# Folded weights kept in DRAM as high and low parts: a hybrid decoder trunk on one Trainium2 core

## The chip, the cores and the metric

The kernel runs on one core of one Trainium2 chip. The metric is the device time of one execution in microseconds. The kernel before took 2501.79 us as the median of 3 runs (2500.89 to 2510.75).

## The reference

One decoder layer on x of 2048 tokens by 1024 columns, in f32, with 256 memory tokens for cross-attention:

```python
mem_n = rmsnorm(mem, mem_norm_g)
h = rmsnorm(x, mix_norm_g)
q, k, v, g, u = split(h @ w_in)                       # 5 x 512 columns
y_ret  = silu(g) * head_rmsnorm(retention(q, k, v))   # 4 heads, chunks of 128, rotary on q and k
y_pool = pool_mixer(u, pool_w, pool_scale)            # 4 groups, causal windows 2/4/8/16, a linear each
x = x + concat(y_ret, y_pool) @ w_out
x = x + cross_attn(rmsnorm(x, xa_norm_g), mem_n, wq, wkv, wo)   # 4 heads of 256
x = x + conv_glu_ffn(rmsnorm(x, ffn_norm_g), w_up, conv_w, conv_b, w_down)
out = rmsnorm(x, final_norm_g)
```

Three products of weights can be made ahead, as the activations come in linearly on one side: wq with the keys of a head (q k^T = h (wq k^T)), the values of a head with wo, and the pooling linear with the rows of w_out behind it. The kernel calls this folding.

## The kernel before, in words

**Tokens and products.** The 2048 tokens are worked in two halves b of T = 1024. Activations lie transposed, 128 columns of the model on the partitions and tokens along the free axis. Every large product has its f32 inputs kept as two f32r numbers, a high and a low part, and takes three matmuls (`passes`, L239: high x high on L241, high x low on L242, low x high on L243). `split` (L230) makes the two parts: a ScalarE copy rounds to the high part (L233, or L236 with a scale), and VectorE subtracts it for the low part (L216, or L225 with a scale). A `unit` (L285) is one output tile of 128 rows by 1024 tokens: it takes a weight tile of 128 x 1024, splits its two halves (`pairs`, L255) and runs 48 matmuls of 512 columns into two PSUM banks, a half weight tile at a time.

**Places.** In SBUF there are five raw tiles R for weights as they are loaded (`new_raw`, L245), three places Q for half a weight tile as a pair (`new_pair`, L250), ten slots T of 576 columns for all kinds of temporaries (`TT`), eight slots Z, and a large arena G for x and 16 further slots (B). PSUM has five banks `mm` for large products and three for the rest (`aux`). A place is taken and freed in program order; the tile framework puts in the waits, by which the next writer of a place stands behind its last reader. A transfer out of a place is a reader too, until it has landed.

**Order.** The framework's scheduler orders the instructions of the whole program by a simulated timeline; each engine then works its own queue in that order. Transfers are issued from SP's queue (nearly all loads), ScalarE's (stores of results) and POOL's. The sums of feed-forward weights (`weight_sums`, L903) are made in DRAM beside the rest by transfers from SP and POOL.

**Folding** (`folded_weights`, L360) is a generator that runs beside the first half's mixing, a piece at a time between the units of a retention head (L1518, L1521). After the projections of the memory to keys and values:
- Md (L460 to L478): for each head, four products of 512 columns (two tiles of 256) of wq^T and keys, 12 matmuls of 256 columns each. ScalarE scales them out of PSUM into a slot of T (L472) and `keep` (L431) stores the slot to DRAM, 256 KB. 16 such tiles.
- VWd (L480 to L496): for each head, four products of 512 columns, 6 matmuls each, of values and wo; evacuated on L490 and stored by `keep`. 16 tiles.
- WPd (L504 to L516): for each pooling group, two products of 512 columns of the pooling linear and its rows of w_out; L511 and `keep`. 8 tiles.

**Use.** Behind the four heads and the pooling groups comes the out-projection (L1534): eight units, whose weight tile is half w_out (L1536) and half WPd (L1537), loaded into the two halves of one raw tile. Then `attention` (L822): `load_m` (L830) loads Md, 512 KB at a time for two tiles, and splits them into two regions of G and Z, except for the first two tiles, whose pairs lie in Q; the products with M, the softmax on tiles of 128 tokens and transposes (L850) follow. Then eight units with VWd (L1576), each a load of 512 KB by `load_tile` (L303) that is split by the unit. Both halves of the tokens load all three again.

Of the kernel before, what the change touches and what calls it, by code (L numbers as in the profile page):

```python
# [8 lines left out]
F32 = mybir.dt.float32  # L9
# [6 lines left out]
P = 128  # L16
# [103 lines left out]
def trunk(ctx, tc, xT, memT, pos, w_qkgu, w_v, wkv, wqT, wo, wout_r, wout_p, poolT, w_up, w_dn, vecs, consts, outT):  # L120
# [72 lines left out]
    Md = drp.tile([2, KT, P, SUB], F32, tag="Md", name="Md")  # L193
    VWd = drp.tile([KT, P, KT, P], F32, tag="VWd", name="VWd")
    rope_d = drp.tile([2, P, SUB], F32, tag="rope_d", name="rope_d")
    WPd = drp.tile([KT, P, 4, P], F32, tag="WPd", name="WPd")
# [67 lines left out]

    def rsqrt(y, v):

        t = small(v.shape[1])
        ts(dve, y.bitcast(I32), v.bitcast(I32), -0.5, ALU.mult, 1597463007.0, ALU.add)
        for _ in range(3):
            tt(dve, t, y, y, ALU.mult)  # L270
            stt(t, t, -0.5, v, ALU.mult, ALU.mult)
            stt(y, t, 1.5, y, ALU.add, ALU.mult)
# [12 lines left out]
    def unit(raw, rhs, evac, order=range(4)):  # L285


        hs = pairs(raw)
        ps = [mmps() for _ in range(NS)]
        for h in range(2):  # L290
            for s in range(NS):
                for j, kk in enumerate(order):
                    k = 4 * h + kk
                    w = [hs[h][:, i, kk * P : (kk + 1) * P] for i in range(2)]
                    passes(ps[s], w, rhs(k, s), h + j == 0, h == 1 and j == 3)
                next(behind[0], None)
                quarter[0] += 1
                if not slow[0] or quarter[0] % 2:
                    next(under[0], None)
                if h == 1:  # L300
                    evac(s, ps[s])
# [58 lines left out]
    def folded_weights():  # L360
# [70 lines left out]
        def keep(dst, t, n):  # L431
            act.dma_start(dst, t.f[:, :SUB].rearrange("p (n c) -> p n c", n=n))
            t.free()

        def tiles4(d, nh, k):
            return d[4 * nh : 4 * nh + 4, :, k, :].rearrange("n p c -> p n c")
# [23 lines left out]
        for h in range(HEADS):  # L460
            dp = [row_pairs(wqT[(2 * h + dt) * P : (2 * h + dt + 1) * P, :]) for dt in range(2)]
            for k2 in range(KT // 2):
# [6 lines left out]
                t = TT.take()  # L469
                for j in range(2):  # L470
                    k = 2 * k2 + j
                    act.activation(t.f[:, j * NMEM : (j + 1) * NMEM], ps[:, j * NMEM : (j + 1) * NMEM], AF.Identity, scale=xag[:, k : k + 1])  # L472
                keep(Md[h // 2, 2 * k2 : 2 * k2 + 2, :, (h % 2) * NMEM : (h % 2 + 1) * NMEM].rearrange("k p m -> p k m"), t, 2)
# [6 lines left out]
        for h in range(HEADS):  # L480
            dp = [row_pairs(wo[(2 * h + dt) * P : (2 * h + dt + 1) * P, :]) for dt in range(2)]
            for mt in range(2):
                for nh in range(2):
# [5 lines left out]
                    t = TT.take()  # L489
                    act.activation(t.f[:, :SUB], ps, AF.Identity, scale=rn[:, mt : mt + 1])  # L490
                    keep(tiles4(VWd, nh, 2 * h + mt), t, 4)
# [12 lines left out]
        for g in range(4):  # L504
            u = row_pairs(wout_p[g])
            for nh in range(2):
# [3 lines left out]
                t = TT.take()  # L510
                act.activation(t.f[:, :SUB], ps, AF.Copy)  # L511
                keep(tiles4(WPd, nh, g), t, 4)
# [309 lines left out]
    def attention(sums, beside, pace):  # L822
# [7 lines left out]
        def load_m(hp):  # L830

            out = mw[hp]
            for kp in range(KT // 2):
                raw = new_raw()
                fetched[0] = sp.dma_start(raw.rearrange("p (k n) -> p k n", k=2), Md[hp, 2 * kp : 2 * kp + 2].rearrange("k p n -> p k n"))
                if hp == 0 and kp == 0:

                    out += [(pr[:, 0], pr[:, 1]) for pr in pairs(raw)]
                    yield
                    continue  # L840
                for i in range(2):
                    u = third[2 * hp].r[:, (2 * kp + i) * T : (2 * kp + i + 1) * T]
                    split(raw[:, i * SUB : (i + 1) * SUB], u[:, :SUB], u[:, SUB:])
# [655 lines left out]
    for b in range(NB):  # L1499
# [34 lines left out]
        for n in range(KT):  # L1534
            raw = new_raw()
            sp.dma_start(raw[:, :SUB], wout_r[n].rearrange("p k c -> p (k c)"))  # L1536
            fetched[0] = sp.dma_start(raw[:, SUB:], WPd[n].rearrange("p k c -> p (k c)"))  # L1537
# [30 lines left out]
        for n in range(KT):  # L1568
# [7 lines left out]
            unit(load_tile(VWd[n]), rhs, add_residual(b, n, xs, acc=acc[n]))  # L1576
# [150 lines left out]
```

## Time and profile before

| | |
|---|---|
| median of 3 runs | 2501.79 us (2500.89 to 2510.75) |
| profiled execution, device time | 2506.72 us |
| its span, first to last instruction | 2504.9 us |
| granted TensorE clock, mean | 0.992 |
| TensorE (PE) busy | 2442.7 us |
| VectorE (DVE) busy | 1666.9 us |
| ScalarE (ACT) busy | 1216.1 us |
| GpSimd (POOL) busy | 652.4 us |
| moved by the DMA engines | 474.28 MB, 189 GB/s on average |

The profile is that of one execution. Its lines name an engine, a source line (L472 is line 472 of the kernel), the tiles written and read ("T<-mm" writes T from a bank mm), and times in microseconds or, where noted, nanoseconds. A helper's line, such as L216 or L233, stands for all who call it, so the tiles tell them apart. Md is stored at 144.7 to 222.2 us of the span and VWd at 250.9 to 289.9; the loads of Md are issued from 421.2 and those of VWd from 465.9 in the first half of the tokens, and the last of VWd in the second half at 1133.8. The feed-forward part takes the rest of the span.

### The profile page before, as it was taken

How to read it: one execution, taken by the hardware profiler on the slowest of the kernel's cores; microseconds unless marked ns; L12 is line 12 of the kernel's file. 1: busy time of each engine (PE TensorE's matmuls, PEld its weight loads, DVE VectorE, ACT ScalarE, POOL GpSimd, SP SyncE). 2: the span in 40 equal slices, each digit the busy share in tenths (PEclk: the TensorE clock that was granted, in tenths of full speed). 3: DMA queues.
4: the chain of work that ended last, by engine and by line, in shares of the span. 5: the costliest groups of instructions: out<-in, count | busy, mean ns of one | idle time of the engine just before them, and what ended most of it. 6: DMA issues, size and time to landing. Idle time of an engine off the chain costs nothing.

```text
span 2504.9 us, 33172 instructions
## 1 busy us (share of the span) xinstructions
PE 2442.7 (98%) x11390; PEld 2037.7 (81%) x11390; DVE 1666.9 (67%) x2574; ACT 1216.1 (49%) x2163; POOL 652.4 (26%) x579
## 2 busy tenths in 40 slices
PE   6999999999999999999999999999999999999997
PEld 6888887788788888888887888878888887888885
DVE  8646566564635675574678776886677586867875
ACT  6333423343321223434654555665555576666663
POOL 1010122100121120030237352553335154222322
PEclk9999999999999999999999999999999999999998
DMA  8363888715766764366567564755556468768951
GB/s 318 89 168 110 244 191 233 234 40 181 227 152 145 159 158 149 111 221 220 167 205 270 166 203 153 236 192 165 160 160 213 136 220 287 250 185 280 346 164 68
DMA packets 257177, 474.28 MB, mean 189 GB/s; under 512 B 26864, under 2 KB 56176, under 8 KB 257008
## 3 DMA queue, kind: packets, MB, share of 16 engines
q1 hardware_dynamic: 212336, 408.18, 49.0%
q0 software_dynamic: 19584, 34.61, 8.9%
q10 hardware_dynamic: 25088, 29.37, 3.4%
q8 instruction: 89, 1.46, 0.2%
q14 instruction: 80, 0.66, 0.1%
HBM read 370.87 MB, written 170.39 MB: 216 GB/s over the span
## 4 chain that ended last, share of the span: by engine, by line
PE 78%; DMA 8%; DVE 6%; issue 3%; POOL 2%; ACT 2%; SPq 0%; POOLq 0%; ACTq 0%; DVEq 0%
PE mm L241 25%; PE mm L242 24%; PE mm L243 24%; POOL T L216 1%; DVE Z L216 1%; DMA T<-Xd 1%; DVE Z L225 1%; DVE G L216 1%; DMA T<-xT 1%; DVE Q L216 1%; DVE T L216 1%; DMA T<-Gd 1%; POOL Z L216 1%; PE aux L749 1%; DMA R<-VWd 0%
## 5 line engine op out<-in xcount | busy, mean ns | idle before, releaser
L241 PE MATMUL mm<-G,Q 128*128 128x512 f32 (+1 forms) x1888 | 728.1, 386 | 21.8 <-ACT Q L233 11.1
L243 PE MATMUL mm<-G,Q 128*128 128x512 f32 (+1 forms) x1888 | 725.9, 385 | 4.4 <-DVE Q L216 4.2
L242 PE MATMUL mm<-G,Q 128*128 128x512 f32 (+1 forms) x1888 | 725.7, 385 | 0.7 <-DVE G L216 0.7
L241 PE MATMUL mm<-G 128*128 128x512 f32 (+1 forms) x1380 | 532.1, 387 | 10.0 <-DVE Z L216 6.3
L242 PE MATMUL mm<-G 128*128 128x512 f32 (+1 forms) x1380 | 531.7, 386 | 0.0
L243 PE MATMUL mm<-G 128*128 128x512 f32 (+1 forms) x1380 | 531.1, 385 | 0.0
L241 PEld LDWEIGHTS mm<-G,Q 128*128 128x128 f32 x1888 | 357.8, 190 | 91.1 <-ACT Q L233 11.8
L243 PEld LDWEIGHTS mm<-G,Q 128*128 128x128 f32 x1888 | 357.7, 190 | 74.3 <-DVE Q L216 5.9
L242 PEld LDWEIGHTS mm<-G,Q 128*128 128x128 f32 x1888 | 358.0, 190 | 69.4 <-DVE G L216 1.6
L225 DVE SCALAR_TENSOR_TENSOR Z<-Z,vecs 128x1024 f32<-128x1024 f32 x176 | 276.3, 1572 | 153.5 <-ACT Z L1069 145.3
L241 PEld LDWEIGHTS mm<-G 128*128 128x128 f32 x1380 | 260.4, 189 | 64.5 <-DVE Z L216 8.0
L243 PEld LDWEIGHTS mm<-G 128*128 128x128 f32 x1380 | 260.2, 189 | 51.8
L242 PEld LDWEIGHTS mm<-G 128*128 128x128 f32 x1380 | 260.1, 188 | 51.5
L1006 ACT ACTIVATE G<-R 128x512 fp32r<-128x512 f32 (+1 forms) x272 | 166.5, 615 | 197.8 <-PE mm L242 178.6
L216 DVE TENSOR_TENSOR Z<-Z,mm 128x512 f32<-128x512 f32 x284 | 192.8, 679 | 78.2 <-PE mm L243 78.0
L216 DVE TENSOR_TENSOR Q<-R,Q 128x512 fp32r<-128x512 f32 x199 | 148.6, 748 | 143.4 <-ACT Q L233 138.9
L216 POOL TENSOR_TENSOR G<-R,G 128x512 fp32r<-128x512 f32 (+1 forms) x100 | 141.9, 1420 | 376.2 <-ACT G L1006 290.9
L233 ACT ACTIVATE Q<-R 128x512 fp32r<-128x512 f32 x150 | 93.8, 627 | 234.8 <-PE mm L242 187.3
L1006 ACT ACTIVATE Q<-R 128x512 fp32r<-128x512 f32 (+1 forms) x204 | 125.0, 613 | 90.9 <-PE mm L242 73.5
L216 DVE TENSOR_TENSOR G<-R,G 128x512 fp32r<-128x512 f32 (+1 forms) x168 | 131.5, 794 | 46.7 <-ACT G L233 38.0
L216 DVE TENSOR_TENSOR G<-T,G 128x512 fp32r<-128x512 f32 (+1 forms) x168 | 125.4, 758 | 53.9 <-ACT G L955 40.7
L940 ACT ACTIVATE aux<-R 128x512 f32<-128x512 f32 (+1 forms) x184 | 105.8, 576 | 95.8 <-DVE Q L216 52.9
(222 smaller groups left out, 2911.4 us busy)
## 6 DMA issues: line engine op xcount, KB each, us to landing
R<-Ud SPq DMA_DIRECT2D x176, 256.0 KB, 2.7
T<-Gd SPq DMA_DIRECT2D x168, 256.0 KB, 4.1
R<-w_up SPq DMA_DIRECT2D x132, 256.0 KB, 3.1
Gd<-Z SPq DMA_DIRECT2D x110, 256.0 KB, 2.4
Ud<-w_up SPq DMA_DIRECT2D x88, 256.0 KB, 5.9
R<-w_qkgu SPq DMA_DIRECT2D x32, 512.0 KB, 4.4
R<-Dd SPq DMA_DIRECT2D x64, 256.0 KB, 4.0
Gd<-T SPq DMA_DIRECT2D x56, 256.0 KB, 3.1
```

Source lines behind the costliest of these rows:

```text
L216: return eng.tensor_tensor(out=out, in0=a, in1=b, op=op)
L225: dve.scalar_tensor_tensor(out=out, in0=a, scalar=s, in1=b, op0=op0, op1=op1)
L233: act.activation(hi, src, AF.Copy)
L241: pe.matmul(ps, lh, rh, start=start, stop=False, skip_group_check=more)
L242: pe.matmul(ps, lh, rl, start=False, stop=False, skip_group_check=more)
L243: pe.matmul(ps, ll, rh, start=False, stop=stop, skip_group_check=more)
L749: pe.matmul(col(self.kv, c), col(self.kn.f, c), self.ch(v, c, h * T), start=True, stop=True)
L940: act.activation(t, x, AF.Copy)
L1006: act.activation(p2[:, 0, :w], self.raw[i].f[:, :w], AF.Copy)
```

## The change

The split is moved from behind the loads to ahead of the stores. `keep` now takes the PSUM bank, splits it into two slots of T (ScalarE the high part, VectorE the low part, both from PSUM; for Md in two halves, as each has a scale of its own) and stores both slots. Md, VWd and WPd hold pairs in DRAM, twice the bytes. `load_m` loads each M tile's pair, 512 KB, straight into the region or place where the product reads it; the VWd units load two pairs of 512 KB straight into Q, and the out-projection loads its WPd half as a pair into Q and splits only its half of w_out. `unit` takes a list of pairs as it is.

```diff
@@ -190,10 +190,10 @@
     t.free()
     dve.memset(phalo, 0.0)
 
-    Md = drp.tile([2, KT, P, SUB], F32, tag="Md", name="Md")
-    VWd = drp.tile([KT, P, KT, P], F32, tag="VWd", name="VWd")
+    Md = drp.tile([2, KT, P, 2, SUB], F32, tag="Md", name="Md")
+    VWd = drp.tile([KT, 2, P, 2, 4, P], F32, tag="VWd", name="VWd")
     rope_d = drp.tile([2, P, SUB], F32, tag="rope_d", name="rope_d")
-    WPd = drp.tile([KT, P, 4, P], F32, tag="WPd", name="WPd")
+    WPd = drp.tile([KT, P, 2, 4, P], F32, tag="WPd", name="WPd")
 
     def mmps():
         return mmp.tile([P, SUB], F32, tag="mm", name=nm("mm"))
@@ -262,6 +262,11 @@
             out.append(pr)
         return out
 
+    def load_pair(src):
+        pr = new_pair()
+        fetched[0] = sp.dma_start(pr.bitcast(F32), src)
+        return pr
+
     def rsqrt(y, v):
 
         t = small(v.shape[1])
@@ -285,7 +290,7 @@
     def unit(raw, rhs, evac, order=range(4)):
 
 
-        hs = pairs(raw)
+        hs = raw if isinstance(raw, list) else pairs(raw)
         ps = [mmps() for _ in range(NS)]
         for h in range(2):
             for s in range(NS):
@@ -428,12 +433,17 @@
                 split(raw[:, i * SUB : (i + 1) * SUB], u.r[:, i * SUB : (i + 1) * SUB], u.r[:, T + i * SUB : T + (i + 1) * SUB])
             return u
 
-        def keep(dst, t, n):
-            act.dma_start(dst, t.f[:, :SUB].rearrange("p (n c) -> p n c", n=n))
-            t.free()
-
-        def tiles4(d, nh, k):
-            return d[4 * nh : 4 * nh + 4, :, k, :].rearrange("n p c -> p n c")
+        def keep(dsts, ps, n, g=None):
+
+            two = [TT.take() for _ in range(2)]
+            hi, lo = (t.f[:, :SUB].bitcast(F32R) for t in two)
+            w = SUB // n
+            for j in range(n if isinstance(g, list) else 1):
+                at = slice(j * w, (j + 1) * w) if isinstance(g, list) else slice(0, SUB)
+                split(ps[:, at], hi[:, at], lo[:, at], g[j] if isinstance(g, list) else g)
+            for t, dst in zip(two, dsts):
+                act.dma_start(dst, t.f[:, :SUB].rearrange("p (n c) -> p n c", n=n))
+                t.free()
 
         kk = B.take(4)
         kp4 = kk.r.rearrange("p (n i m) -> p n i m", i=2, m=NMEM)
@@ -466,11 +476,8 @@
                         k = 2 * k2 + j
                         w = [dp[dt].r[:, i * T + k * P : i * T + (k + 1) * P] for i in range(2)]
                         passes(ps[:, j * NMEM : (j + 1) * NMEM], w, (kp4[:, 2 * h + dt, 0], kp4[:, 2 * h + dt, 1]), dt == 0, dt == 1)
-                t = TT.take()
-                for j in range(2):
-                    k = 2 * k2 + j
-                    act.activation(t.f[:, j * NMEM : (j + 1) * NMEM], ps[:, j * NMEM : (j + 1) * NMEM], AF.Identity, scale=xag[:, k : k + 1])
-                keep(Md[h // 2, 2 * k2 : 2 * k2 + 2, :, (h % 2) * NMEM : (h % 2 + 1) * NMEM].rearrange("k p m -> p k m"), t, 2)
+                to = Md[h // 2, 2 * k2 : 2 * k2 + 2, :, :, (h % 2) * NMEM : (h % 2 + 1) * NMEM]
+                keep([to[:, :, i].rearrange("k p m -> p k m") for i in range(2)], ps, 2, [xag[:, 2 * k2 + j : 2 * k2 + j + 1] for j in range(2)])
             for u in dp:
                 u.free()
             if h == HEADS - 1:
@@ -486,9 +493,8 @@
                         lh = [vp4[:, 2 * h + dt, i, mt * P : (mt + 1) * P] for i in range(2)]
                         w = [dp[dt].r[:, i * T + nh * SUB : i * T + (nh + 1) * SUB] for i in range(2)]
                         passes(ps, lh, w, dt == 0, dt == 1)
-                    t = TT.take()
-                    act.activation(t.f[:, :SUB], ps, AF.Identity, scale=rn[:, mt : mt + 1])
-                    keep(tiles4(VWd, nh, 2 * h + mt), t, 4)
+                    to = VWd[4 * nh : 4 * nh + 4, h // 2, :, :, 2 * (h % 2) + mt]
+                    keep([to[:, :, i].rearrange("n p c -> p n c") for i in range(2)], ps, 4, rn[:, mt : mt + 1])
             for u in dp:
                 u.free()
             if h == HEADS - 1:
@@ -507,9 +513,8 @@
                 ps = mmps()
                 lh = [pw.r[:, i * SUB + g * P : i * SUB + (g + 1) * P] for i in range(2)]
                 passes(ps, lh, [u.r[:, i * T + nh * SUB : i * T + (nh + 1) * SUB] for i in range(2)], True, True)
-                t = TT.take()
-                act.activation(t.f[:, :SUB], ps, AF.Copy)
-                keep(tiles4(WPd, nh, g), t, 4)
+                to = WPd[4 * nh : 4 * nh + 4, :, :, g]
+                keep([to[:, :, i].rearrange("n p c -> p n c") for i in range(2)], ps, 4)
             u.free()
             if g == 3:
                 pw.free()
@@ -831,16 +836,13 @@
 
             out = mw[hp]
             for kp in range(KT // 2):
-                raw = new_raw()
-                fetched[0] = sp.dma_start(raw.rearrange("p (k n) -> p k n", k=2), Md[hp, 2 * kp : 2 * kp + 2].rearrange("k p n -> p k n"))
-                if hp == 0 and kp == 0:
-
-                    out += [(pr[:, 0], pr[:, 1]) for pr in pairs(raw)]
-                    yield
-                    continue
-                for i in range(2):
-                    u = third[2 * hp].r[:, (2 * kp + i) * T : (2 * kp + i + 1) * T]
-                    split(raw[:, i * SUB : (i + 1) * SUB], u[:, :SUB], u[:, SUB:])
+                for k in (2 * kp, 2 * kp + 1):
+                    if hp == 0 and kp == 0:
+                        pr = load_pair(Md[hp, k])
+                        out.append((pr[:, 0], pr[:, 1]))
+                        continue
+                    u = third[2 * hp].r[:, k * T : (k + 1) * T]
+                    fetched[0] = sp.dma_start(u.bitcast(F32), Md[hp, k].rearrange("p i n -> p (i n)"))
                     out.append((u[:, :SUB], u[:, SUB:]))
                 yield
 
@@ -1534,7 +1536,9 @@
         for n in range(KT):
             raw = new_raw()
             sp.dma_start(raw[:, :SUB], wout_r[n].rearrange("p k c -> p (k c)"))
-            fetched[0] = sp.dma_start(raw[:, SUB:], WPd[n].rearrange("p k c -> p (k c)"))
+            pr = new_pair()
+            split(raw[:, :SUB], pr[:, 0], pr[:, 1])
+            raw = [pr, load_pair(WPd[n].rearrange("p i k c -> p i (k c)"))]
             got, ahead = ahead, fetch_x(b, n + 1) if n + 1 < KT else None
             unit(raw, lambda k, s: (mix[k].r[:, s * SUB : (s + 1) * SUB], mix[k].r[:, T + s * SUB : T + (s + 1) * SUB]), add_residual(b, n, xs, got=got), (0, 2, 3, 1))
         for u in mix:
@@ -1573,7 +1577,7 @@
                 at = (k % 4) * T + s * SUB
                 return tuple(prob[k // 4].r[:, i * 4 * T + at : i * 4 * T + at + SUB] for i in range(2))
 
-            unit(load_tile(VWd[n]), rhs, add_residual(b, n, xs, acc=acc[n]))
+            unit([load_pair(VWd[n, h].rearrange("p i k c -> p i (k c)")) for h in range(2)], rhs, add_residual(b, n, xs, acc=acc[n]))
             act.dma_start(Xd[b, n], acc[n].f)
             if b + 1 < NB:
                 load_x(n, nxt, got)
```

## The prediction

> **What bounds the kernel now.** I read the page's first part, then the whole list of TensorE's waits, then the stretches in which TensorE idles.
>
> ```profile
> span 2504.9 us, 33172 instructions
> ...
> PE 2442.7 (98%) x11390; PEld 2037.7 (81%) x11390; DVE 1666.9 (67%) x2574; ACT 1216.1 (49%) x2163; POOL 652.4 (26%) x579
> ```
> TensorE is busy for 2442.7 of 2504.9 us, so 62.2 us are idle in all. The change leaves the matmuls as they are; it can save a part of those 62 us, or add to them.
>
> ```profile
> engine line waited for: us in total, times, longest us
> PE mm L241 <- ACT Q L233: 11.1, 4, 9.0
> ...
> PE aux L850 <- DVE T L220: 4.5, 2, 4.3
> ...
> PE aux L777 <- DVE T L216: 0.8, 2, 0.5
> PE mm L242 <- DVE G L216: 0.7, 1, 0.7
> PE mm L241 <- ACT T L490: 0.3, 1, 0.3
> PE aux L749 <- ACT T L744: 0.2, 1, 0.2
> ```
> Each row is an engine and line, what it waited for, the sum, the number of times and the longest. The 11.1 us lie at the very start and are not touched. Around the folding (100 to 340 us) TensorE waits only for the last rows, 0.5 + 0.3 + 0.2 = 1.0 us: today's folding is all but free. The 4.3 us of L850 are the entry of attention of the first half of the tokens, and those the change can reach:
>
> ```profile
> 500.96 1.11 PE L850 MATMUL aux<-consts,T 128*128 128x128 f32 x4 [4.34 <-DVE T L220]
> ...
> 502.30 0.63 PE L243 MATMUL mm<-G 128*128 128x512 f32 x1
> 502.73 0.63 PE L241 MATMUL mm<-G 128*128 128x512 f32 x1
> ...
> 504.12 0.39 PE L242 MATMUL mm<-G 128*128 128x512 f32 x1
> 504.35 0.39 PE L243 MATMUL mm<-G 128*128 128x512 f32 x1
> ```
> ```profile
> 481.77 12.46 DMA R<-VWd
> ```
> ```profile
> ACT Q L233 <- DMA R<-VWd: 11.2, 1, 11.2
> ```
> The chain of waits says why: a load of VWd takes 12.46 us, ScalarE stands before its split for 11.2 us in its in-order queue, and the exponentials of the softmax are queued behind it. After the gap TensorE starts matmuls every 0.43 us instead of 0.23 for about 3 us, which costs some seven matmuls at 0.2, 1.5 us more.
>
> **The change part by part.** Durations first; columns are the group, busy us and mean ns of one, then idle before it by releaser.
>
> ```profile
> L490 ACT ACTIVATE T<-mm,rnm 128x512 f32<-128x512 f32 x16 | 10.9, 687 | 11.4 <-DMA VWd<-T 6.6 <-PE mm L243 2.2 <-ACT T L490 1.4
> L472 ACT ACTIVATE T<-mm,vecs 128x256 f32<-128x256 f32 x32 | 13.3, 473 | 6.0 <-PE mm L243 3.7 <-PE aux L777 2.2
> L225 DVE SCALAR_TENSOR_TENSOR T<-aux,vecs,T 128x512 f32<-128x512 f32 x6 | 4.5, 750 | 1.5 <-PE aux L777 1.4
> L225 DVE SCALAR_TENSOR_TENSOR T<-T,aux 128x128 f32<-128x128 f32 x14 | 4.0, 284 | 0.4
> L233 ACT ACTIVATE G<-R 128x512 fp32r<-128x512 f32 x41 | 24.7, 629 | 22.9 <-DMA R<-wout_p 8.2 <-DMA R<-wo 7.8 <-PE mm L242 4.6
> L216 DVE TENSOR_TENSOR Q<-R,Q 128x512 fp32r<-128x512 f32 x25 | 17.2, 690 | 42.2 <-ACT Q L233 42.0
> ```
> ```profile
> Md<-T ACTq DMA_DIRECT2D x16, 256.0 KB, 2.8
> ```
> ```profile
> R<-Md SPq DMA_DIRECT2D x8, 512.0 KB, 5.6
> R<-VWd SPq DMA_DIRECT2D x5, 512.0 KB, 13.7
> ```
> ```profile
> L432 ACTq DMA_DIRECT2D VWd<-T x16: 366/366/519, 250.9 to 289.9; - x16
> ...
> DMA to landing us min/median/max: 2.3/5.7/17.2
> ```
>
> *Work moved.* Removed are the splits after the loads: 32 for Md, 32 for VWd, 16 for WPd, each one ScalarE operation of 0.63 us and one VectorE operation of 0.69: 50 and 55 us on engines that are 49% and 67% busy. Added in the folding are 32 low parts of 256 columns for Md (no row has this shape; between 0.28 of 128 and 0.75 of 512 columns I take the middle, 0.45), 16 for VWd at 0.75 and 8 for WPd at 0.69: 32 us of VectorE. ScalarE's evacuations stay (L490, L472, L511); it issues 40 more stores, 40 x 0.37 = 15 us. None of this is on TensorE, so it counts only where TensorE waits for it: at three bursts of fold products, at two entries, and at the loads.
>
> *The folding.* A fold product is 6 matmuls of 512 columns (12 of 256 for Md), 6 x 0.23 = 1.4 us, into one of five PSUM banks. Before, one ScalarE operation freed the bank. Now the VectorE low part behind it frees it, and each product takes two slots of the ten of T, each freed only when its store has landed. In the built order of the changed kernel I followed each such wait:
> - Md of the last head: the first product after the head's transposes needs the bank whose low part stands behind a gating operation (0.75), a query split (0.69), half a low part (0.45), the other half's high part (0.47), and its own end (0.45): 2.8, and 0.5 for hand-overs: 3.3 us. Two products later a rotation's VectorE operation waits for a slot whose store was issued 2.8 us (landing) before, about 1; a further bank about 1. **5 us**, from 3 to 7.
> - VWd, first burst of eight: the high part of the fourth product waits for the landing of the second's store, out of the same slot. From the second's high part: 0.69, issue 0.37, landing 5.7, then high 0.69 and low 0.75 = 8.2 us, in which TensorE has 1.44 us of waiting for the previous low part and then one product and four transposes, 1.9: about 4.9 us idle. The next two products wait for low parts queued on VectorE, about 1 more, and the slowed matmuls after a gap of 4.9 us cost 1.5, as behind the gap at 500.96. **7.5 us**. Its 5.7 is the median of the last row (VWd's stores and loads). With 2.3, the least there, the gap is 1.5 and there is no slow stretch: 2.5. With twice the median it is 13.
> - VWd, second burst: its slots have a head's whole unit more; nothing unless a landing passes 8 us.
> - WPd: five products in a row wait for low parts that stand among the last head's rotation and gating, some behind a landing. By the same queues **4 us**, from 1 to 6.
>
> Sum 16.5, less the 1.0 us of waits that stand there today: +15.5.
>
> How long those stores take decides most of it. The Trainium skill ("DMA: Bandwidth & Descriptors", section "Latency and other measured facts") puts a fixed cost of about 2 us on a small DMA. By it the VWd burst would cost 2.5 and the sum fall by 5; the median row of 5.7 us speaks against it, under the load of this stretch, and the sum goes by the row.
>
> *Entry of attention, first half.* With no split of VWd or Md left, ScalarE doesn't stand before a load there: the 4.3 us gap and its 1.5 us of slow matmuls go, **-5.8**. What is late next: eight 512 KB loads of M pairs for the first two heads go into places that come free as the last out-projection unit ends, 32 to 100 matmuls (7 to 23 us) before their use, at 5.6 us each in the row above, up to several in flight; I take +1.8 (0 to 4). Net **-4**.
>
> *Pool and out-projection, first half.*
>
> ```profile
> 373.64 7.30 DMA Ud<-w_up
> ...
> 384.51 0.49 POOL T L630
> ```
> ```profile
> 385.00:390.00 5.00, 4.46 (x19) 3.14 (x17) 4.88 (x8) 0.00 (x0) 2.55 (x4) 1.00 0.48 56
> 390.00:395.00 5.00, 1.77 (x7) 1.17 (x8) 5.00 (x11) 1.75 (x3) 1.13 (x2) 1.00 1.00 295
> ...
> 620.00:640.00 20.00, 20.00 (x90) 16.57 (x89) 10.94 (x17) 7.66 (x13) 4.15 (x5) 1.00 0.92 229
> ```
> After the stretch and its length stand the busy times of PE, PEld, DVE, ACT and POOL, the granted clock, the share of the DMA engines and GB/s. At 385 to 395 TensorE is busy 6.23 of 10 us: 3.8 idle. The chain runs from a weight sum's transfer (Ud) to POOL's pooling copies (L630), which stand behind the sums in POOL's queue. In the built order fewer sums are ahead of them (28 of their first transfers instead of 40), so most of it goes; but the WPd pairs are twice the bytes and Q holds three, not five, tiles. **-2** (-4 to +3).
>
> *Later loads.* Q's three places let a VWd pair be asked for one unit (48 matmuls, 11 us) ahead; before, five places of R. A 512 KB load within 11 us is in time by the 5.6 us row and late by the 13.7 us row; at 620 to 640 the DMA engines are 0.92 busy, and 4 MB more in the 88 us of this stage (8 units) is 48 GB/s. I take **+1** (0 to 21, the latter 8 units x (13.7 - 11.1)). In the second half the first WPd pair has 22 matmuls, 5 us: **+1.5** (0 to 4).
>
> **Sum:** 15.5 - 4 - 2 + 1 + 1.5 = **+12 us**. The profiled execution took 2506.72 us of device time (1.8 around its span), so 2518.7 like for like; the median of the runs is 2501.79, 4.93 below it, and 2513.8 on that scale. The prediction is **2513.8**, slower by 0.48%.
>
> **The rivals.**
> 1. *The bursts are absorbed and the stall goes: not slower.* If stores land in 2.3 us and the scheduler's interleaving leaves TensorE other work, the folding costs 1 to 3 and -5.8 and -2 stand: -3 to -8, at about 2497. For it: VectorE is 67% busy over the span, and today's folding waits for 1.0 us. Against: five banks, and ten slots that carry rotation and retention as well. It decides from a landing under about 3 us.
> 2. *Pair loads come late.* Double bytes and three places: 8 units x 2.6 = 21 us on top of the forecast, about 2534. For it: 13.7 us and 0.92 busy; against: 13.7 us is the row of five loads asked for close together as attention begins; later ones are spread one unit apart.
> 3. *Nothing that counts.* The removed splits lay beside matmuls, the added low parts do too: within 3 us of before.
> 4. *The clock.* In the Trainium skill ("TensorE: Matmul & The Clock Gate", "What's actually happening") an idle gap of about 3.4 us or more halves TensorE's clock until it has been busy for as long again. The row at 500.96 agrees: 4.34 us idle, then 0.43 us spacing. If the three bursts each pause for over 4.3 us, two more slow stretches of 1.5 us come: +15, about 2517. This lies within the forecast's spread.
>
> **How the numbers follow.** Forecast (with rival 4), from +4 to +24: 0.58, of which 0.25 lies under +12.5. Rival 1: 0.20, of which 0.06 is beyond -12.5. Rival 2: 0.15. Rival 3: 0.07. About 0.5%, 12.5 us, is what a measurement of this kernel can tell from no change; so faster 0.06, same 0.25 + 0.14 + 0.07 = 0.46, slower 0.33 + 0.15 = 0.48. The range runs from -7 (part of rival 1's cases) to +33 (rival 2): 2495 to 2535.
>
> **What would show it.** Right: TensorE's list of waits gains rows for VectorE low parts of fold products (L225 out of mm) or of rotations at 215 to 335 us, some 16 us in all, with stores of VWd and Md behind them; the row of L850 behind L220 with 4.3 us and ScalarE's wait for VWd are gone; 385 to 395 has more than 8 us of matmuls. Wrong: TensorE's waits in the folding stay under 5 us; or TensorE waits for DMAs into Q in the unit loops (rival 2); or the added waits lie elsewhere, in the feed-forward stage for instance, whose order of work the scheduler may have moved.

## The result, and the profile after

The changed kernel takes 2566.67 us (median of 5 runs, 2562.81 to 2573.16), the kernel before 2500.89 (5 runs, 2497.74 to 2510.75): a ratio of 1.0258, 95% interval 1.0231 to 1.0284. It is 66 us slower; forecast was 12 (2513.8 against 2501.79), in a range that ended at 2535.

The page of the profiled execution of the changed kernel (device time 2562.81 us) opens so:

```profile
span 2561.0 us, 33151 instructions
...
PE 2460.4 (96%) x11390; PEld 2046.6 (80%) x11390; DVE 1652.0 (65%) x2550; ACT 1170.8 (46%) x2081; POOL 658.1 (26%) x579
...
DMA packets 276762, 505.75 MB, mean 197 GB/s; under 512 B 28017, under 2 KB 73713, under 8 KB 276593
```
ScalarE does 45 us less and VectorE 15 us less, as the change means to do. TensorE's idle time rose from 62.2 to 2561.0 - 2460.4 = 100.6 us, and its busy time by 17.7 us for the same 11390 matmuls: it ran at a lower clock more often (granted clock 0.984 instead of 0.992 on average). 38.4 + 17.7 = 56.1 us is the whole difference of the two spans.

To see where, take two landmarks that both kernels have: the last store of WPd (the end of the folding) and the first store of x (Xd) behind a VWd unit. Their rows give first and last start; first the kernel before, then the changed one.

```profile
L432 ACTq DMA_DIRECT2D WPd<-T x8: 366/366/562, 314.8 to 332.6; - x8
```
```profile
L1577 ACTq DMA_DIRECT2D Xd<-Z x16: 326/326/327, 592.7 to 1205.0; - x16
```
```profile
L445 ACTq DMA_DIRECT2D WPd<-T x16: 366/366/1308, 333.8 to 358.2; - x16
```
```profile
L1581 ACTq DMA_DIRECT2D Xd<-Z x16: 326/326/349, 646.2 to 1262.3; - x16
```

| part | before | changed | difference |
|---|---|---|---|
| start to last WPd store (folding) | 332.6 | 358.2 | +25.6 |
| from there to the first x store behind VWd (pooling, first out-projection, entry of attention) | 260.1 | 288.0 | +27.9 |
| from there to the last such store (the other VWd units and the second half of the tokens) | 612.3 | 616.1 | +3.8 |
| the rest of the span (feed-forward) | 1299.9 | 1298.7 | -1.2 |

So nearly all of it arises before 650 us, in two parts of about equal size. The first landmark does not cut the work at quite the same place: 1751 matmul instructions lie ahead of it in the changed kernel and 1742 in the one before, and at 0.23 us each for those of 512 columns the 9 more are about 2 us that belong to the second part. In the folding the changed kernel's matmuls show these gaps (in brackets: idle before, and what ended it):

```profile
216.78 0.55 PE L241 MATMUL mm<-G 128*128 128x256 f32 x1 [4.50 <-DVE T L225]
...
219.69 0.41 PE L242 MATMUL mm<-G 128*128 128x256 f32 x1
219.90 0.41 PE L243 MATMUL mm<-G 128*128 128x256 f32 x1
...
220.54 0.28 PE L241 MATMUL mm<-G 128*128 128x256 f32 x1
220.66 0.28 PE L242 MATMUL mm<-G 128*128 128x256 f32 x1
...
263.00 0.50 PE L241 MATMUL mm<-G 128*128 128x512 f32 x1 [1.75 <-DVE T L225]
...
267.25 0.65 PE L782 MATMUL aux<-consts,T 128*128 128x128 f32 x4 [2.58 <-DVE T L216]
...
272.34 0.79 PE L241 MATMUL mm<-G 128*128 128x512 f32 x1 [4.44 <-DVE T L225]
...
277.62 0.63 PE L241 MATMUL mm<-G,Q 128*128 128x512 f32 x1
278.05 0.51 PE L242 MATMUL mm<-G,Q 128*128 128x512 f32 x1
278.39 0.39 PE L243 MATMUL mm<-G,Q 128*128 128x512 f32 x1
278.63 0.39 PE L241 MATMUL mm<-G,Q 128*128 128x512 f32 x1
```
The first is the Md burst, the next three the first VWd burst. Behind the Md gap matmuls of 256 columns come 0.21 us apart instead of 0.12, until 220.12. Behind the last of the VWd burst those of 512 columns come 0.43 us apart until 278.05, so the slow stretch lasts 5.7 us. In the second part it is the first out-projection and the statistics behind it:

```profile
429.15 0.79 PE L241 MATMUL mm<-G,Q 128*128 128x512 f32 x1 [5.49 <-DMA Q<-WPd]
...
461.29 0.79 PE L241 MATMUL mm<-G,Q 128*128 128x512 f32 x1 [7.23 <-ACT Q L233]
...
489.94 0.79 PE L241 MATMUL mm<-G,Q 128*128 128x512 f32 x1 [3.31 <-DMA Q<-WPd]
499.55 0.50 PE L241 MATMUL mm<-G,Q 128*128 128x512 f32 x1 [2.28 <-ACT Q L233]
...
530.65 1.84 PE L320 MATMUL aux<-consts,T 128*128 128x1 f32 x8 [5.24 <-DVE T L216]
```
The gap of 4.34 us at L850 is gone, and larger ones ahead of it have come. The transfers in 390 to 545 us of the changed kernel (number, size, median from issue to landing) and the busy share of the DMA engines in two stretches:

```profile
Ud<-w_up SPq DMA_DIRECT2D x43, 256.0 KB, 11.0
Ud<-w_up POOLq DMA_DIRECT2D x22, 256.0 KB, 8.2
Ud<-Ud POOLq DMA_DIRECT2D x22, 256.0 KB, 12.0
Q<-WPd SPq DMA_DIRECT2D x8, 512.0 KB, 13.9
```
```profile
450.00:460.00 10.00, 4.07 (x18) 3.02 (x17) 1.98 (x3) 1.26 (x2) 1.63 (x2) 0.96 1.09 286
460.00:470.00 10.00, 8.71 (x29) 7.00 (x30) 3.28 (x5) 2.41 (x4) 1.63 (x2) 0.70 1.04 323
```
The last two numbers are the busy share and GB/s: the engines are full (shares a little above 1 stand so in the profile), and a WPd pair that Q's places ask for 11 us ahead takes 13.9. The largest group of transfers is not the pairs at all but the sums of feed-forward weights (Ud), of which the kernel before issues fewer there: 24 from SP in 370 to 500 us, a stretch 25 us shorter.

```profile
Ud<-w_up SPq DMA_DIRECT2D x24, 256.0 KB, 6.3
```
From one landmark to the other it is 36 before and 44 in the changed kernel; between the first and the last WPd load of the changed kernel stand 29. The chain of waits from a WPd load to a matmul that waits for one (start, length, what) runs through SP's queue:

```profile
415.25 13.86 DMA Q<-WPd
...
429.17 12.74 DMA T<-xT
...
441.92 12.42 DMA Ud<-w_up
...
454.36 11.76 DMA Ud<-w_up
...
467.32 7.78 DMA Ud<-w_up
...
475.93 13.97 DMA Q<-WPd
...
489.94 0.79 PE mm L241
```
By these rows, whose releasers the profile infers, SP stands until one transfer has landed before it issues the next, though a load of x (xT) does not read a WPd pair, nor a sum a load of x. In 390 to 545 us SP waits for landings for about 100 of 155 us; in the kernel before, in 370 to 500, for 28 of 130. So a late transfer also delays the next ones in SP's order. How much of the lateness comes from the bytes and how much from this order was not separated by a run.

### The profile page after: what moved, and what is told of

The parts are those of the page before. It is cut to its first block, busy times and chain, and to the rows that moved or that the text cites. A ratio compares the mean times of both kernels' runs of the same rounds, so it can differ in the third digit from the quotient of the medians.

```text
span 2561.0 us, 33151 instructions
## 1 busy us (share of the span) xinstructions
PE 2460.4 (96%) x11390; PEld 2046.6 (80%) x11390; DVE 1652.0 (65%) x2550; ACT 1170.8 (46%) x2081; POOL 658.1 (26%) x579
## 4 chain that ended last, share of the span: by engine, by line
PE 77%; DMA 11%; DVE 5%; issue 3%; POOL 2%; ACT 2%; SPq 1%; POOLq 0%; ACTq 0%; DVEq 0%
PE mm L241 24%; PE mm L242 24%; PE mm L243 24%; DMA T<-xT 2%; DMA Ud<-w_up 2%; POOL T L216 1%; DMA Q<-WPd 1%; DVE Z L216 1%; DVE T L216 1%; DVE G L216 1%; DVE Z L225 1%; DMA VWd<-T 1%; POOL Z L216 1%; DMA T<-Xd 1%; PE aux L743 1%
## 5 line engine op out<-in xcount | busy, mean ns | idle before, releaser
L216 DVE TENSOR_TENSOR Q<-R,Q 128x512 fp32r<-128x512 f32 x147 | 112.0, 763 | 99.7 <-ACT Q L233 88.3
L216 DVE TENSOR_TENSOR G<-T,G 128x512 fp32r<-128x512 f32 (+1 forms) x171 | 131.4, 779 | 62.9 <-ACT G L957 40.5
L216 DVE TENSOR_TENSOR T<-T 128x512 f32<-128x512 f32 (+4 forms) x153 | 107.6, 713 | 75.2 <-ACT T L360 59.9
L216 DVE TENSOR_TENSOR G<-R,G 128x512 fp32r<-128x512 f32 (+1 forms) x156 | 125.7, 817 | 33.1 <-ACT G L233 22.2
```

The source lines that it names most:

```text
L216: return eng.tensor_tensor(out=out, in0=a, in1=b, op=op)
```

## The experiments

Two theories of the out-projection were tried first. **S**: the weight sums, which the scheduler now puts more densely into this part, fill the DMA engines, and everything waits for its bytes. **P**: the WPd pairs themselves, twice as large and through three places of Q, come late. "Stage" below is the time from the last WPd store to the first x store behind VWd. All ratios are to the kernel before on the same chip. Parts and stages are read from one profiled execution each, while executions of one kernel differ by up to 15 us in all (no_low from 2541.17, the profiled one, to 2556.57): a few us between two stages say little.

**One of the three pairs at a time**, and the changed kernel without low parts.

```diff
 md_only:  keep() and load_m as changed; VWd and WPd stored and loaded as before
 vw_only:  VWd alone as changed          wp_only:  WPd alone as changed
```


> Only Md is split ahead of its stores and loaded as pairs; VWd and WPd as in the kernel before. In the built order 32 transfers of weight sums stand between the first and last load of WPd (20 in the kernel before, 29 in the changed one). Theory S (the first out-projection is slow because more of the weight sums' transfers stand in it and fill the DMA engines): out-projection stalls of over 8 us remain, though WPd is loaded as before; 15 to 30 us slower than before. Theory P (it is slow because the WPd pairs are 512 KB each and Q has three places): no stall there, only Md's burst in the folding (about 4.5 us) and M loads: 3 to 10 us slower.

> Only VWd is split ahead of its stores and loaded as pairs. Both theories: the burst in the folding of about 9 us at 260 to 275 us of the span and little in the out-projection, where 20 transfers of sums stand as in the kernel before; the wait of 4.3 us at the entry of attention gone or replaced; 5 to 15 us slower than before. If VWd's pairs come late in their units: over 20.

> Only WPd is split ahead of its stores and loaded as pairs. 24 transfers of sums stand between the first and the last load of WPd. Theory P: TensorE waits for loads of Q from WPd and for splits of w_out behind them, 15 us or more: 18 to 35 us slower than before. Theory S: about 3 us in the folding and under 5 us in the out-projection: 3 to 9 us slower.

| | median us | ratio (95%) | folding ends | stage |
|---|---|---|---|---|
| md_only | 2520.57 | 1.0064 (1.0042 to 1.0086) | 339.7 (+7.1) | 262.9 |
| vw_only | 2529.40 | 1.0103 (1.0077 to 1.0129) | 346.4 (+13.8) | 262.4 |
| wp_only | 2521.26 | 1.0071 (1.0050 to 1.0091) | 340.7 (+8.1) | 260.2 |

The costs in the folding add up: 29.0 against 25.6 together, or some 22 against 24 when the matmuls ahead of the landmark are counted alike (14 more than in the kernel before in vw_only, 16 more in wp_only). The stage doesn't: each alone leaves it at 260 to 263 us. TensorE's waits in wp_only from 390 to 545 us:

```profile
PE aux L320 <- DVE T L216: 6.8, 2, 6.5
PE mm L241 <- DMA Q<-WPd: 3.3, 3, 1.4
```
Late WPd pairs alone cost 3.3 us, so theory P in its simple form is out. md_only stalls 8.1 us in the out-projection though its WPd is loaded as before, as S expected, but the stage as a whole is only 2.8 us longer. vw_only (24.7 us over the kernel before) and wp_only (16.6) came out slower than S had them, and not in the stage: their foldings cost 13.8 and 8.1 us instead of 9 and 3, some 3 and 4 of it by those additional matmuls, and from the first to the last x store behind VWd they take 7.5 and 5.3 us more than the kernel before (619.8 and 617.6 against 612.3). For vw_only more than 20 us was to mean VWd pairs that come late in their units; the trace has one such wait of 4.17 us, at 1151.48.

```diff
 no_low, in keep():
-            two = [TT.take() for _ in range(2)]
...
-                split(ps[:, at], hi[:, at], lo[:, at], ...)
...
+            t = TT.take()
...
+                act.activation(hi[:, at], ps[:, at], AF.Identity, scale=...)   # Copy for WPd
+            for dst in dsts:  # one slot, stored twice
+                act.dma_start(dst, t.f[:, :SUB]...)
```


> The changed kernel without the low parts in the folding: one ScalarE operation evacuates each product into one slot, which is stored twice (the low part that is loaded is thus not the low part). Loads as in the changed kernel. Both theories: the 14 to 16 us of waits of TensorE for low parts and slots at 215 to 355 us go, with some 3 us of slow clock behind them: 15 to 22 us faster than the changed kernel, still 40 to 50 slower than before, as 28 transfers of sums and the pairs of WPd still meet in the out-projection.

2553.92 us, 1.0198 (1.0181 to 1.0216), 15 us less than the changed kernel by the two ratios (0.6%); the last WPd store at 342.9, so 15.3 of the 25.6 us are gone and 10.3 stay. But 25 more matmuls stand ahead of that landmark than in the kernel before (1767 against 1742), which is 5 to 6 us of the 10.3: with no low part in sight, 40 more stores cost some 5 us. The stage stays at 285.3, with those 25 matmuls fewer in it.

**The sums taken out of the out-projection**, in the changed kernel and in the one before.

```diff
 after_hold, before_hold:
+        if b == 0:
+            under, paused = [iter(())], under
         for n in range(KT):
             raw = new_raw()
...
+        if b == 0:
+            under = paused
         for u in mix:
             u.free()
```


> The changed kernel with the generator of the weight sums not called in the eight units of the first out-projection, so that they are made up later. In the built order 9 of their SP transfers stand between the first and last WPd load (29 in the changed kernel) and none between there and the first VWd load. Measure: from the last WPd store to the first store behind a VWd unit, 288 us in the changed kernel, 260 in the one before. Theory S (sums flood the DMA engines in this stage): 260 to 270. Theory P (places of Q and 512 KB pairs): still over 280. The total can get worse at other places, where the sums then stand.

> The kernel before with the same edit: the control. The stage from the last WPd store to the first store behind a VWd unit stays at 255 to 262 us by both theories; the total within 10 us of before.

The stage falls from 288.0 to 253.8 us in the changed kernel, further than S had it, and from 260.1 to 252.1 in the one before, where both theories had it stay; with the sums out, the two kernels differ by 1.7 us (12 matmuls fewer lie in the stage of after_hold, so 4 to 5 at equal work). Pairs of twice the size and three places of Q, without the sums beside them, thus do not make the stage long: P is out. after_hold's total is 2574.43 us, 1.0271 (1.0253 to 1.0289): the sums now meet the second half's WPd and VWd, where a wait for a WPd pair of 10.80 us stands at 992.99, and from the first to the last x store behind VWd it takes 658.8 us instead of 616.1. before_hold is 2501.61, 0.9986 (0.9975 to 0.9997): the only version here that beats the kernel before, and only by 0.14%. The stage of both, in one row each (share of the DMA engines and GB/s last):

```profile
360.20:614.00 253.80, 247.99 (x1158) 204.08 (x1157) 136.98 (x295) 76.85 (x169) 24.40 (x35) 1.00 0.55 175
```
```profile
333.70:585.80 252.10, 249.34 (x1170) 207.26 (x1169) 152.88 (x323) 90.57 (x197) 24.27 (x28) 1.00 0.42 131
```

**Two of the pairs, and more places.**

```diff
 md_wp:  Md and WPd as changed, VWd as before
 q4:
-    R = cp.tile([P, 5 * T], F32, tag="R", name="R")
-    Q = cp.tile([P, 3 * T], F32R, tag="Q", name="Q")
+    R = cp.tile([P, 4 * T], F32, tag="R", name="R")
+    Q = cp.tile([P, 4 * T], F32R, tag="Q", name="Q")
...
```


> Md and WPd as pairs, VWd as in the kernel before. Each alone left the stage from the last WPd store to the first store behind a VWd unit at 260 to 263 us, all three together 288. Theory S, by bytes of pairs and sums together: 21 transfers of sums in the out-projection against 29, so 265 to 280. Theory P: Q's places are short as soon as WPd's pairs and M's first two pairs go through them: 280 to 288.

> The changed kernel with four places of Q instead of three and four raw tiles instead of five (in the feed-forward part eight raw halves instead of ten and one more pair). Stage from the last WPd store to the first store behind a VWd unit: theory P 260 to 270 us; theory S, with the DMA engines full in this stage and 37 transfers of sums in the out-projection, 280 to 290. The feed-forward part may change by some us.

md_wp: 2540.42 us, 1.0137 (1.0118 to 1.0156), stage 274.7, as S expected. It has no more sums in the stage than the kernel before (36 from SP): with as many sums, the pairs of Md and WPd make it 14.6 us longer. q4: 2589.71 us, 1.0326 (1.0294 to 1.0357), stage 293.9: a fourth place, taken from the raw tiles, doesn't help, and with 37 transfers of sums in the out-projection the stage is the longest of all. As q4 changes the places, the raw tiles and the sums at once, it does not tell by itself what a place is worth; after_hold does.

**More sums in the kernel before, fewer in the changed one.**

```diff
 before_more, in unit():
                     next(under[0], None)
+                    for _ in range(more_sums[0] * (quarter[0] % 2)):   # more_sums[0]: 1 in the first out-projection, else 0
+                        next(under[0], None)
 after_half:
-        slow[0] = False      # ahead of the out-projection
...
+        slow[0] = False      # behind it
```


> The kernel before with an extra step of the weight sums in every second quarter of a unit of the first out-projection: 32 of their SP transfers between first and last WPd load and 8 to the first VWd load (20 and 8 in the kernel before, 29 and 4 in the changed one); loads as before. If the sums alone fill the DMA engines and stop TensorE: the stage from the last WPd store to the first store behind a VWd unit at 275 us or more (260 before, 288 in the changed kernel). If it takes the doubled bytes of the pairs with them: 258 to 268.

> The changed kernel with the weight sums stepped in every second quarter in the first out-projection and attention entry's units, as in the heads before (slow set to False behind the out-projection instead of ahead): 21 and 0 transfers instead of 29 and 4. By theory S the stage from the last WPd store to the first store behind a VWd unit lies between 254 (none) and 288: 262 to 275.

before_more: 2522.29 us, 1.0081 (1.0061 to 1.0100), stage 276.9. The sums alone, with no pair anywhere, make the stage 16.8 us longer. after_half: 2567.77 us, 1.0257 (1.0236 to 1.0278), stage 268.6, between the two ends as expected; the second half gives the gain back (8.31 us of waiting for a WPd pair at 1061.26). The rows of the kernel before, of before_more and of the changed kernel:

```profile
332.60:592.70 260.10, 251.71 (x1170) 208.05 (x1169) 152.56 (x323) 93.09 (x198) 35.87 (x52) 0.99 0.63 175
```
```profile
335.80:612.70 276.90, 257.94 (x1171) 212.50 (x1170) 152.45 (x323) 90.51 (x197) 48.27 (x68) 0.96 0.73 195
```
```profile
358.20:646.20 288.00, 261.60 (x1162) 214.01 (x1161) 136.26 (x296) 74.98 (x167) 46.38 (x59) 0.94 0.66 198
```

**The folding by itself.**

```diff
 keep_only: keep() as changed; load_m, unit(VWd) and the out-projection read [.., 0, ..] as f32 into R and split it
 keep_pool, in keep() of keep_only:
-                split(ps[:, at], hi[:, at], lo[:, at], ...)
+                act.activation(f[:, at], ps[:, at], ...)      # f32, into lo's slot
+            pool.tensor_copy(hi, f)
+            tt(pool, lo, f, hi.bitcast(F32), ALU.subtract)
 keep_one, in keep() of keep_only:
-            for t, dst in zip(two, dsts):
-                act.dma_start(dst, t.f[:, :SUB]...)
+            act.dma_start(dsts[0], two[0].f[:, :SUB]...)
...
 keep_hold: keep_only with the edit of before_hold
```


> The folding of the changed kernel, with pairs split out of PSUM and stored, but the loads of the kernel before: they load the high part alone (256 KB, as f32) and split it again, so the low part is left out of the products. The weight sums stand exactly where they stand in the kernel before (28, 20, 8). The last WPd store comes at 355 to 360 us (332.6 before), and behind it the stage to the first store behind a VWd unit takes 258 to 264 us: in all 22 to 30 us slower than before. If the loads of the changed kernel are what slows the folding, 333 to 340.

> As keep_only, but ScalarE evacuates each product into a slot of T in f32 and GpSimd makes both parts from there, so that a PSUM bank is free after one ScalarE operation, as in the kernel before; two slots and two stores as in the changed kernel. Theory B (TensorE waits since the banks are held until VectorE's low part): the last WPd store at 333 to 342 us. Theory L (it waits since the slots of T are held until the stores have landed): still over 350.

> As keep_only (loads of the kernel before, of the high part), and the low part, though still made by VectorE out of PSUM into its own slot, is not stored: 40 stores instead of 80, a slot of low parts is free at once. The last WPd store is at 360.4 us in keep_only and 332.6 in the kernel before. If the waits of the folding come from slots held by stores that have not landed: 335 to 346. If they come from PSUM banks held until VectorE's low part: 350 to 358.

> As keep_only, with the weight sums not stepped in the first out-projection (0 and 0 of their transfers there instead of 20 and 8). keep_only took 271.1 us from the last WPd store to the first store behind a VWd unit, 11 more than the kernel before with as many sums and bytes. If sums that come later than the slower folding allows for still are the reason: 252 to 256, as in before_hold. If the folding itself leaves something behind in that stage: over 260.

| | median us | ratio (95%) | folding ends | stage |
|---|---|---|---|---|
| keep_only | 2546.10 | 1.0175 (1.0156 to 1.0195) | 360.4 (+27.8) | 271.1 |
| keep_pool | 2584.58 | 1.0321 (1.0296 to 1.0345) | 403.1 (+70.5) | 270.3 |
| keep_one | 2528.14 | 1.0094 (1.0077 to 1.0112) | 340.1 (+7.5) | 269.1 |
| keep_hold | 2533.25 | 1.0111 (1.0095 to 1.0126) | 360.2 (+27.6) | 254.5 |

keep_only shows that the folding's cost is that of `keep` alone: with the loads of before it is as large (360.4, a little behind the 355 to 360 expected). Its total was missed (44 us over the kernel before in place of 22 to 30): the stage behind took 271.1 us instead of 258 to 264. keep_hold shows that the sums make that difference too, as without them the stage is 254.5. keep_pool failed as a test: making both parts on GpSimd is slower by itself (9.05 us of TensorE waiting at 351.28), and whether the banks count is not told by it. keep_one tells it: with VectorE's low parts made in the same way, and the banks held as long, but 40 stores fewer, 20.3 of the 27.8 us go. At an equal count of matmuls ahead of the landmark (1735 in keep_one, 1756 in keep_only) it is some 16 of 25, so low parts without their stores cost about 9 us, stores without low parts (no_low) about 5, and both together about 24. Neither does it alone. keep_one also takes 40 issues off ScalarE's queue, 40 x 0.37 = 15 us of it; what they cost beside the held slots was not separated.

```profile
L444 ACTq DMA_DIRECT2D WPd<-T x8: 366/366/367, 319.3 to 340.1; - x8
```
Among the waits behind it, in the changed kernel from 140 to 364 us, are these for landings:

```profile
PE mm L241 <- DVE T L225: 10.7, 3, 4.5
ACT T L236 <- DMA VWd<-T: 9.2, 3, 5.6
DVE T L216 <- DMA Md<-T: 9.1, 5, 3.6
DVE T L225 <- DMA VWd<-T: 6.8, 4, 4.3
```
TensorE waits for VectorE's low parts (first row), and ScalarE and VectorE for slots of T whose stores of VWd and Md have not landed (the others).

**The stage against what is moved in it**, from the rows of all runs:

| | MB in the stage | sums issued by SP | clock | stage us |
|---|---|---|---|---|
| before_hold | 32.95 | 12 | 1.00 | 252.1 |
| keep_hold | 32.87 | 12 | 0.99 | 254.5 |
| after_hold | 44.37 | 20 | 1.00 | 253.8 |
| before | 45.56 | 36 | 0.99 | 260.1 |
| keep_only | 45.37 | 36 | 0.97 | 271.1 |
| keep_one | 45.36 | 36 | 0.97 | 269.1 |
| keep_pool | 43.41 | 29 | 0.94 | 270.3 |
| wp_only | 47.61 | 36 | 0.98 | 260.2 |
| md_only | 49.73 | 36 | 0.98 | 262.9 |
| vw_only | 50.30 | 44 | 0.97 | 262.4 |
| after_half | 50.72 | 32 | 0.97 | 268.6 |
| md_wp | 51.73 | 36 | 0.96 | 274.7 |
| before_more | 53.94 | 52 | 0.96 | 276.9 |
| changed | 57.02 | 44 | 0.94 | 288.0 |
| no_low | 57.08 | 44 | 0.95 | 285.3 |
| q4 | 57.38 | 44 | 0.93 | 293.9 |

Up to some 45 MB the stage can be as short as 252 to 254 us; from 50 MB it grows by about 4 us for each MB ((288.0 - 262.4) / (57.02 - 50.30) = 3.8), a rough line that after_half and md_wp miss by 5 to 7 us. The count of sums alone does not order the rows: vw_only has as many as the changed kernel and stays at 262.4. before has 45.56 MB and the changed kernel 11.46 more: 8 more transfers of sums by SP and 8 by POOL (16 x 0.26 = 4.2 MB); the rest, some 7 MB, is mostly pairs, with 2.6 MB of loads of w_v and w_qkgu that also moved into the stage. keep_only, keep_one and keep_pool take 9 to 11 us longer than before with no more bytes; keep_hold puts it down to the sums for keep_only. In keep_only the largest gap of the stage, 6.01 us at 406.62, stands behind a chain that runs from a sum's landing (Ud<-Ud, issued at 370.85) over POOL's further sums to a pooling copy (L635) at 397.08, as the gap at 385 to 395 did in the kernel before; no run changes this alone.

## Why the prediction was wrong

- **Md burst, +5.** Right in place and size: a gap of 4.50 us, and 0.69 ahead of it. The slow stretch behind it, 3.3 us and so about 1.5 us more, was left out of the sum; rival 4 had it.
- **VWd burst, +7.5.** The gaps are 1.75 + 2.58 + 4.44 = 8.8 us; the chain was the one followed (the slots wait for stores), with a median landing of 4.8 us instead of 5.7. The slow stretch behind lasts 5.7 us instead of 3: at 0.43 instead of 0.23 it costs 5.7 x 0.20 / 0.43 = 2.7 us instead of 1.5.
- **WPd, +4.** Gaps of 0.73, 0.76, 0.36 and 0.55 us: 2.4.
- **Folding in sum, +15.5 forecast, +25.6 measured.** The gaps of over 0.3 us from 100 to 360 us sum to 17.9, near what was forecast; that is in part luck, as VWd's gaps came out larger (8.8 where 6 were in the sum) and WPd's smaller (2.4 for 4). What was left out is the slower clock behind them. Two rows of the kernel before and the same of the changed one, with the granted clock in the third column from the end:

```profile
140.00:237.00 97.00, 96.80 (x578) 85.65 (x577) 55.20 (x109) 36.74 (x91) 4.91 (x6) 1.00 0.54 152
237.00:317.00 80.00, 79.15 (x401) 66.63 (x400) 50.60 (x116) 33.49 (x76) 8.90 (x11) 1.00 0.75 207
```
```profile
140.00:237.00 97.00, 91.82 (x535) 81.50 (x534) 63.15 (x132) 35.08 (x81) 4.88 (x6) 0.98 0.64 188
237.00:317.00 80.00, 70.17 (x343) 58.29 (x343) 51.45 (x103) 28.98 (x60) 4.06 (x5) 0.94 0.70 202
```
By the clock that is about 97 x 0.02 + 80 x 0.06 = 6.7 us, against 1.5 forecast. TensorE's busy time up to the landmark says the same: it rose by 9.3 us (from 311.3 to 320.6), of which the 9 more matmuls are 2. Waits of under 0.3 us add only 0.2.
- **Entry of attention, -4.** The removed split did remove its wait: with the sums out of the stage (after_hold) no gap of 0.4 us stands at the entry, while before_hold and keep_hold, which split on the load side, have one of 2.76 us at L850 and one of 5.14 us at L855. In the changed kernel the gain was not to be seen, as the statistics ahead of it (530.65) wait 5.24 us, on a chain that runs through a load of Md of 8.81 us (519.94).
- **Pool and out-projection, -2 (-4 to +3).** This is the step that failed. "In the built order fewer sums are ahead of them (28 of their first transfers instead of 40), so most of it goes" counted the sums that went away from one place and did not ask where they went: into the out-projection, right behind, beside pairs of twice the size. The gap at 385 to 395 did go (TensorE is busy for all of these 10 us in the changed kernel), but the part took 27.9 us more where the sum of this step and the last said 6 less. after_hold and before_hold (253.8 and 252.1) show that the loss needs the sums there, before_more (276.9) that more sums alone make the stage longer, md_wp (274.7) that pairs beside the sums of before do so too. Sums and larger pairs together make the transfers of this part late; whether by full DMA engines or by the order in SP's queue was not separated.
- **Later loads, +2.5.** Right in size: +3.8, with waits of 1.46 us for a WPd pair and 3.22 for a VWd pair in the second half.
- **Rival 2** named late pairs and gave 2534, but put them at the VWd units and at Q's three places; for VWd pairs there were only two waits, 3.4 us in all, the larger (3.22) in the second half. Its sign and its resource, the DMA engines, were right; its place and its cause were not. Rival 1 is wrong, rival 3 is wrong, and rival 4's extra was under-sized: TensorE's busy time rose by 17.7 us over the span.
- **The signs.** Those named for being right came in the main (low parts as releasers in the folding, the row of 4.3 us gone, 385 to 395 full), and so did one named for being wrong: TensorE waits for DMAs into Q in the unit loops, 11.9 us for WPd and 3.4 for VWd.

The two rules of the Trainium skill that the prediction weighed: "DMA: Bandwidth & Descriptors" ("Latency and other measured facts") has a fixed cost of about 2 us for a DMA; the stores here, of 256 KB, landed after 3.4, 4.8 and 3.2 us (medians for Md, VWd and WPd), so the row was the better guide. On the clock, "TensorE: Matmul & The Clock Gate" ("What's actually happening") has the full clock come back after at least one busy window of about 3.4 us; the slow stretches here lasted 3.3 us behind 216.78 and 5.7 behind 272.34, so one window was not always enough.

## What to carry to other kernels

When a built order shows that background transfers have left one place, count them at the place where they have gone, and sum the bytes of that stage against what the stage's length can carry: here some 45 MB in 250 us could be free, and from 50 MB each further MB cost about 4 us. A split that is moved ahead of a store does not only move work: each product then holds two slots until two stores have landed. Here neither the added low parts nor the added stores alone cost more than some 9 us in the folding, and both together about 24. Look at the idle gaps and then add the slow clock behind them, which here was about a third of the whole loss.

## What the runs showed of the hardware

- With the DMA engines at a busy share of 1.04 to 1.09 the core moved 286 to 323 GB/s (two rows of 450 to 470 us), and 310 on average over 390 to 545 us, where a 512 KB load of a WPd pair took a median of 13.9 us to land; loads of that size for Md took 5.6 in the kernel before. The Trainium skill ("DMA: Bandwidth & Descriptors", "Specifications") has about 358 GB/s as the limit of HBM for a core; the average here, with DRAM-to-DRAM sums among the transfers, stays below it, but single slices of 3.9 us in that stretch reach 400.
- TensorE's slow stretch behind a gap was 3 us long behind 4.34 us (kernel before, 500.96), 3.3 us behind 4.50 us (216.78) and 5.7 us behind 4.44 us (272.34), so its length cannot be read from the gap.
- ScalarE's issue of a store, 0.37 us as a rule, took up to 1.6 us among the doubled stores of the changed kernel:

```profile
L445 ACTq DMA_DIRECT2D Md<-T x32: 366/370/1598, 145.9 to 231.7; - x32
```
